# Depthwise convolution of a six-layer kernel: the taps as 128x32 column tiles over token-shifted copies

## The chip, the cores and the metric

The kernel runs on one core of a Trainium2 chip, as one program that computes six layers on 256 tokens. The metric is the time of one execution on the device, in microseconds (us): the median of the runs shown, less is better.

A core has five engines, each with its own queue of instructions that it works off in order: TensorE (PE, matrix products, with PEld for the loads of its stationary operand), VectorE (DVE), ScalarE (ACT), GpSimd (POOL) and SyncE (SP, here used to issue DMAs). They wait for one another by semaphores. Products land in PSUM, in one of eight banks of 128 partitions; everything else lies in SBUF, 128 partitions wide.

## The reference, cut to what matters

The first block has four layers: retention, convolution, dilated attention, retention, each followed by a SwiGLU of 2816 hidden features; a second block of two layers follows. The change touches the second layer alone, its mixer:

```python
def _conv_mixer(h, w_in, b_in, w_dw, b_dw, ln_g, ln_b, w_out, b_out):
    a = h @ w_in + b_in
    u = a[..., :D_MODEL] * jax.nn.sigmoid(a[..., D_MODEL:])
    u = lax.conv_general_dilated(
        u, w_dw[:, None, :].astype(u.dtype), window_strides=(1,), padding=[(CONV_PAD, CONV_PAD)],
        dimension_numbers=('NWC', 'WIO', 'NWC'), feature_group_count=D_MODEL) + b_dw
    u = jax.nn.silu(_layernorm(u, ln_g, ln_b))
    return u @ w_out + b_out
```

D_MODEL is 1024, there are 256 tokens, and the convolution is depthwise with 31 taps: for each channel c and token t the output is the sum over k of w_dw[k, c] * u[t + k - 15, c]. All of it is in 32 bit floating point.

## The kernel before

**Layout.** Activations lie transposed: channels on partitions, in eight chunks of 128, tokens along the free dimension. A weight matrix comes as a stream of 128x128 blocks in the order in which they are used; one DMA on SP's queue fetches 16 of them (`raw`, 1 MB, line 255, three buffers), and for each half tile ACT rounds to a high part (`hi`) and DVE subtracts to get a low part (`lo`). A product of a block is three matmuls (`mmB`, line 320): hi by the high part of x, hi by the low part, lo by the high part, each with 256 columns of fp32r. `_advance` (line 259) keeps the splits four half tiles and the loads five ahead of the half tile that is being used.

**Order.** Nothing is scheduled by a compiler. The program writes each engine's queue itself: a main line of products, and generators beside it (`spawn`, `pump`, `need`) that are resumed after each `mmB` once a planner's estimate of time has passed what they wait for. The planner has a cost for each operation (`Engine.cost`, `Kern.mm`). Where its estimate is wrong the order in the queues stays and the engine waits.

**The convolution layer** (`conv`, line 1056). `kouter` forms the products of w_in for chunks 0 to 2 over all of x; then the main line goes through chunks 3 to 7, 2 x 8 blocks each, that is 48 matmuls of one chunk. Each finished chunk has an `evac` (line 1071): GpSimd clears the padding of a tile `U`, DVE multiplies the products by the norm's factor R (`t`), ACT takes the sigmoid (`sg`), and DVE forms u in `U`, with 15 columns of padding on both sides, eight buffers.

The taps follow. For each chunk, 13 to 16 of the 31 go to TensorE (`TAPS`, line 1053): ACT builds a diagonal 128x128 matrix of the tap's weights for each (`cdg`, line 1098), and a matmul in fp32 of this matrix with `U` shifted by k columns is accumulated in a bank (`taps_pe`, line 1121). An fp32 matmul stands in the trace as two instructions. The other taps go to DVE, each one multiplying and adding along 256 tokens, into two accumulators `cv` and `cacc` in turn (`taps_dve`, line 1128); DVE then adds the two, and `combine` (line 1151) adds the bank.

`stats` (line 1160) subtracts a shift common to all channels, sums the channels and their squares (POOL adds chunk after chunk), and after the last chunk forms the layer norm's factors with PE, DVE and POOL in turn. `act` gives each chunk's silu as a high and a low part (`hh`, `hl`), and the main line goes on with w_out. Between the last tap and w_out, `warm` products, whose result nobody reads, keep PE occupied.

The constants of the channels, the 248 columns of tap weights among them, lie in the tile `V`, loaded at the start in two DMAs on ACT's queue (lines 423 and 438).

Of the kernel before, what the change touches and what calls it, by code (L numbers as in the profile page):

```python
# [19 lines left out]
D = 1024  # L20
# [11 lines left out]
# columns of the per-feature vectors, eight to a vector of 1024  # L32
# [3 lines left out]
def _vec_layout():  # L36
    n = 0
    for i in range(4):
        for j in range(4):
            VEC[f"n{i}{j}"] = n  # L40
            n += 8
    for name, w in (
        ("mix0", 8), ("mix1", 8), ("mlp0", 8), ("mlp1", 8), ("fin", 8),
        ("cb_in", 16), ("cb_dw", 8), ("cln_g", 8), ("cln_b", 8), ("cb_out", 8),
        ("lconv_w", 32), ("lconv_b", 8), ("lb_r", 8), ("lb_i", 8), ("lam", 8),
        ("mnorm", 8), ("subln", 1), ("cw_dw", 248),
    ):
        VEC[name] = n
        n += w
    return n  # L50
# [4 lines left out]
# columns of the scalars that every partition holds  # L55
# [8 lines left out]
def shape_consts():  # L64
# [23 lines left out]
    c["amask"] = mk  # L88
    c["cmask"] = np.where(s[None, :] <= s[:, None], 0.0, BIG).astype(f)
# [23 lines left out]

class Bank:
    """One bank of PSUM while it is held"""
# [8 lines left out]
class Times:  # L124
    """When the parts of the tensors will have been written, by an estimate of what every operation takes"""
# [24 lines left out]
class Engine:  # L150
    """An engine's operations, with the time it will have worked them off"""
# [51 lines left out]
class Kern:  # L203
    def __init__(self, nc, tc, ctx, ap, stop_after=None):
# [11 lines left out]
        # weight stream  # L216
# [6 lines left out]
        # chains beside the main line: [generator, time from which on it may go on]  # L223
# [12 lines left out]
        # whether an operation's start is held to be after the products that were given before it  # L236
# [10 lines left out]
    # ---------------------------------------------------------------- stream  # L247
    PD, PS = 5, 4

    def _load(self, n):  # L250
        """the next tile of the stream, in n pieces"""
# [25 lines left out]
    def blk(self, name, layer, r0, c0, n=1):  # L277
        """The next n 128x128 blocks (side by side along columns) of the stream, high and low part."""
# [13 lines left out]
    # -------------------------------------------------------------- products  # L292
# [6 lines left out]
    def mm(self, out, lhsT, rhs, start, stop):  # L299
# [3 lines left out]
        if rhs.dtype == F32:  # L303
            cost = 4 * max(n, 64) / 2400 if n > 8 else 0.2
        elif rhs.dtype == F32R:
            cost = max(n, 256) / 2400
        else:
            cost = max(n, 64) / 2400
# [7 lines left out]
    def w(self, *aps):  # L316
        """how long it will be until these have been written"""
        return max([self.times.read(x.t if isinstance(x, Bank) else x) for x in aps]) + 0.05 - self.now

    def mmB(self, out, w, xk, start, stop):  # L320
        """out[128 features, T] += block^T x; xk: (high, low) parts of x^T."""
# [7 lines left out]
    def mmA(self, out, w, xk, start, stop):  # L329
        """out[128 tokens, 512] += x block."""  # L330
# [7 lines left out]
    def warm(self, n):  # L338
        """Products that nobody reads, in a pause too short to let the array's clock drop."""
# [6 lines left out]
    # ------------------------------------------------- banks and side chains  # L346
# [61 lines left out]
    # ----------------------------------------------------------------- setup  # L408
# [46 lines left out]
    def log1p_series(self, s, shape, name, terms):  # L455
        """2 atanh(s), s an AP with |s| <= 1/3."""
# [11 lines left out]
    def softplus_tail(self, x, shape, name):  # L468
        """log1p(exp(-|x|))"""
# [11 lines left out]
    def decays(self):  # L481
        """log(1 - exp(l)) of every head, direction and layer"""
# [25 lines left out]
    def decay_tables(self, j, dp):  # L508
        """per head the blocks [later from earlier positions and the reverse; the two blocks on the diagonal]"""
# [16 lines left out]
    # ----------------------------------------------------------------- norms  # L526
# [6 lines left out]
    def sums(self, b, srcs, first, last):  # L533
        """columns 2 i and 2 i + 1 of b: what a sum over the channels of source i adds"""
# [6 lines left out]
    def rms_root(self, tiles, eps, ps):  # L541
        """(mean + eps)^-1/2 per token, tokens on partitions"""
# [13 lines left out]
    def bcast(self, rs, tiles, ps, o=0):  # L556
        """ps[p, t] = rs[t] on every partition"""
# [4 lines left out]
    def prenorm_chunk(self, c, src, gain, T, perm, have=False):  # L562
        """operand parts of src*gain (the high one may be there), and the sum of squares"""
# [21 lines left out]
    def prenorm_finish(self, T, tiles):  # L585
        """sets self.rs (tokens on partitions) and self.R (on every partition)"""
# [34 lines left out]
    def kouter(self, T, outs, key, cut=lambda n: 0):  # L621
        """Products of the first outputs of a projection, one chunk of x after the other.
        outs: (bank, column, first of its bank); key(k, n): block key; cut(n): tokens left out."""
# [17 lines left out]
    def splitp(self, src, T=T2):  # L641
        """high and low part of src (SBUF or PSUM) as tiles"""
# [6 lines left out]
    # ------------------------------------------ post norm of the first block  # L649
    OUT_TILES = ((0, 2), (2, 2), (4, 2), (6, 1), (7, 1))  # L650

    def out_alloc(self):
        """accumulators of the eight output chunks"""
# [17 lines left out]
    def post_begin(self, gain, nk, bias=None):  # L671
        """nk: products that are still to come for each chunk"""
# [6 lines left out]
    def post_chunk(self, c):  # L679
        """after the last product of chunk c"""  # L680
# [37 lines left out]
    def post_copy(self, c0, n, m, on_vector):  # L718
        """m * gain; the last on_vector of them on the vector engine"""
# [15 lines left out]
    def boundary(self, perm, gain2, perm2=False, full=False):  # L735
        """x += m * rstd * gain, then the operand of the next projection: its first chunk here, the others on
        the way (feed)"""
# [52 lines left out]
    def feed(self, n=1):  # L790
        """the next n chunks of the operand"""
# [4 lines left out]
    # ------------------------------------------------------------ first block  # L796
# [14 lines left out]
    def retention(self, i, j):  # L811
# [13 lines left out]
        # heads 0 and 1: queries and keys, one x chunk after the other  # L825
# [226 lines left out]
    # taps of each chunk of channels on the tensor engine  # L1052
    TAPS = (16, 13, 14, 16, 16, 16, 16, 14)
    CD = 1.0

    def conv(self, i, j):
# [8 lines left out]
        ln, U, sums = {}, {}, {}  # L1065
# [5 lines left out]
        def evac(c, b):  # L1071
# [3 lines left out]
            u = self.wk.tile([128, S + 30], F32, name="U", tag="U", bufs=8)  # L1075
# [13 lines left out]
            U[c] = u  # L1089

        def claim():
            """taps for the tensor engine, channel after channel, each with its diagonal matrix"""
            for c in range(KD):
                while c not in U:
                    yield None
                for k in range(self.TAPS[c]):
                    d = self.wk.tile([128, 128], F32, name="cdg", tag="cdg", bufs=8)
                    self.sc.activation(d, self.ident, AF.Copy, scale=self.vec("cw_dw", 8 * k + c))
                    yield c, k, d

        def taps_pe():
            src, ahead, b = claim(), deque(), None
            more = True
            while more or ahead:
                while more and len(ahead) < 4:
                    x = next(src, 0)
                    if x is None:
                        break
                    if x == 0:
                        more = False  # L1110
                    else:
                        ahead.append(x)
                if not ahead:
                    yield 0.3
                    continue
                c, k, d = ahead.popleft()
                last = k == self.TAPS[c] - 1
                if k == 0:
                    b, = yield from self.need(1)
                yield self.w(d, U[c])  # L1120
                self.mm(b[:, :S], d, U[c][:, k:k + S], k == 0, last)
                if last:
                    sums[c] = b
                    self.spawn(combine(c))
                if k % 2:
                    yield 0.0

        def taps_dve():
            for c in range(KD):
                while c not in U:  # L1130
                    yield 0.3
                shifted = "shift" in done
                if shifted:
                    done.add(("shifted", c))
                acc = [cv[:, c], self.wk.tile([128, S], F32, name="cacc", tag="cacc")]
                for n, k in enumerate(range(self.TAPS[c], 31)):
                    w = self.vec("cw_dw", 8 * k + c)
                    x, a = U[c][:, k:k + S], acc[n % 2]
                    if n == 0 and shifted:
                        self.ve.scalar_tensor_tensor(out=a, in0=x, scalar=w, in1=K, op0=ALU.mult, op1=ALU.subtract)  # L1140
                    elif n == 1 and not shifted:
                        self.ve.tensor_scalar(a, x, w, None, ALU.mult)
                    elif n < 2:
                        self.ve.tensor_scalar(a, x, w, self.vec("cb_dw", c), ALU.mult, ALU.add)
                    else:
                        self.ve.scalar_tensor_tensor(out=a, in0=x, scalar=w, in1=a, op0=ALU.mult, op1=ALU.add)
                    yield self.ve.clock - self.now - 0.5
                self.ve.tensor_tensor(acc[0], acc[0], acc[1], ALU.add)
                done.add(c)

        def combine(c):
            while c not in done:
                yield 0.1
            b = sums[c]
            yield self.w(b, cv[:, c]) + (0.0 if c == KD - 1 else self.CD)
            self.ve.tensor_tensor(cv[:, c], cv[:, c], b[:, :S], ALU.add)
# [3 lines left out]
        def stats():  # L1160
            """sums over channels, shifted by the mean of the first two chunks"""
# [89 lines left out]
        self.spawn(taps_pe())  # L1251
# [907 lines left out]
```

## Time and profile before

| | |
|---|---|
| Median of 3 runs | 2451.79 us (2450.5 to 2452.13) |
| Span of the profiled execution, first to last instruction | 2449.6 us |
| PE busy | 2398.2 us, 98 % of the span |
| DVE, ACT, POOL busy | 67 %, 47 %, 9 % |
| Mean granted TensorE clock | 0.998 |
| DMA | 384 MB read from HBM, 157 GB/s over the span |

The profiled execution's own span is 2.2 us under the median. The span runs from the first to the last instruction; what lies around it is in the run's time and not in the span. A matmul's end is modelled and lies after the start of the next one, so the pitch, from one start to the next, is what a stream of matmuls takes, and PE's busy share is not a measure of how well PE is used.

### The profile page before, as it was taken

The page shows a single profiled execution, that of the slowest core. Times are in us where ns is not written, and L with a number is a line of the kernel's source. Part 1 is how long each engine was busy: PE and PEld are TensorE (multiplying, and loading weights), DVE is VectorE, ACT ScalarE, POOL GpSimd, SP SyncE. Part 2 cuts the span into 40 slices and gives each one's busy share as a digit, 9 for nine tenths or more (in the row PEclk, how much of TensorE's full clock was granted, in tenths as well). Part 3 has the DMA queues.
Part 4 walks back from the last instruction along what each step waited for, and adds up shares of the span by engine and source line. Part 5 has one row for each costly group of instructions (what it writes and reads, how often), then busy time and mean ns, then how long its engine had stood idle before and what let it go on. Part 6 is the DMA issues. An engine that isn't in the chain of part 4 may idle for free.

```text
span 2449.6 us, 43712 instructions
## 1 busy us (share of the span) xinstructions
PE 2398.2 (98%) x18193; PEld 2284.9 (93%) x18193; DVE 1653.0 (67%) x2826; ACT 1162.2 (47%) x1879; POOL 224.1 (9%) x284
## 2 busy tenths in 40 slices
PE   7999999999999999999999999999999999999998
PEld 7889999989998989989998899999999999989998
DVE  7556756898567758777567557566776756586764
ACT  5544543665434444444445444344765444356443
POOL 1002001112002000020011002002000100131000
PEclk9999999999999999999999999999999999999999
DMA  6443553304554433325544453544343445433552
GB/s 240 161 172 125 214 184 138 146 34 161 190 184 156 152 141 136 116 108 211 186 149 176 155 186 144 205 173 161 135 154 138 157 170 182 168 112 113 206 190 104
DMA packets 56935, 387.89 MB, mean 158 GB/s; under 512 B 7360, under 2 KB 8128, under 8 KB 10656
## 3 DMA queue, kind: packets, MB, share of 16 engines
q1 hardware_dynamic: 53280, 381.18, 43.0%
q10 hardware_dynamic: 3200, 2.99, 0.4%
q8 instruction: 143, 2.34, 0.4%
q0 software_dynamic: 256, 0.92, 0.1%
q14 instruction: 56, 0.46, 0.1%
HBM read 384.02 MB, written 1.05 MB: 157 GB/s over the span
## 4 chain that ended last, share of the span: by engine, by line
PE 87%; DVE 6%; POOL 3%; issue 2%; ACT 2%; DMA 0%; ACTq 0%; SPq 0%; DVEq 0%; POOLq 0%
PE b L310 84%; DVE lo L198 2%; PE b L314 2%; POOL X L198 1%; ACT hi L198 1%; DVE cv L198 1%; POOL acc L198 1%; DVE xl L198 1%; DVE cacc L198 1%; POOL rs L198 1%; DVE xh L198 0%; PE b L343 0%; DVE ptmp L198 0%; DMA raw<-in_w 0%; DVE X L198 0%
## 5 line engine op out<-in xcount | busy, mean ns | idle before, releaser
L198 DVE TENSOR_TENSOR lo<-raw,hi 128x1024 fp32r<-128x1024 f32 (+1 forms) x723 | 876.6, 1235 | 278.7 <-ACT hi L198 278.6
L310 PE MATMUL b<-xh,hi 128*128 128x256 f32 (+1 forms) x3272 | 937.6, 290 | 14.3 <-ACT hi L198 9.3
L310 PE MATMUL b<-xl,hi 128*128 128x256 f32 (+1 forms) x3272 | 916.7, 284 | 4.3 <-DVE xl L198 4.1
L310 PE MATMUL b<-xh,lo 128*128 128x256 f32 (+1 forms) x3272 | 913.4, 283 | 0.9 <-DVE lo L198 0.9
L198 ACT CAST hi<-raw 128x1024 fp32r<-128x1024 f32 (+1 forms) x723 | 738.8, 1044 | 281.3 <-PE b L310 241.9
L310 PEld LDWEIGHTS b<-xh,hi 128*128 128x128 f32 x3272 | 611.2, 188 | 25.2 <-ACT hi L198 9.5
L310 PEld LDWEIGHTS b<-xl,hi 128*128 128x128 f32 x3272 | 611.0, 188 | 8.9 <-DVE xl L198 6.7
L310 PEld LDWEIGHTS b<-xh,lo 128*128 128x128 f32 x3272 | 613.4, 189 | 1.1 <-DVE lo L198 1.1
L310 PE MATMUL b<-hh,hi 128*128 128x256 f32 (+1 forms) x1792 | 511.1, 285 | 0.6 <-ACT hh L198 0.6
L310 PE MATMUL b<-hl,hi 128*128 128x256 f32 (+1 forms) x1792 | 507.4, 283 | 0.5 <-DVE hl L198 0.2
L310 PE MATMUL b<-hh,lo 128*128 128x256 f32 (+1 forms) x1792 | 507.1, 283 | 0.0
L310 PEld LDWEIGHTS b<-hh,hi 128*128 128x128 f32 x1792 | 337.5, 188 | 2.5 <-issue 0.9
L310 PEld LDWEIGHTS b<-hl,hi 128*128 128x128 f32 x1792 | 337.2, 188 | 1.7 <-DVE hl L198 1.3
L310 PEld LDWEIGHTS b<-hh,lo 128*128 128x128 f32 x1792 | 337.4, 188 | 0.0
L198 DVE TENSOR_TENSOR t<-b,R 128x512 f32<-128x512 f32 x96 | 65.4, 689 | 208.2 <-PE b L310 206.5
L310 PE MATMUL b<-hi,xh 128*128 128x512 f32 x352 | 142.2, 404 | 0.5 <-DVE xh L198 0.5
L310 PE MATMUL b<-lo,xh 128*128 128x512 f32 x352 | 140.0, 398 | 0.3 <-DVE lo L198 0.3
L310 PE MATMUL b<-hi,xl 128*128 128x512 f32 x352 | 139.6, 396 | 0.0
L198 ACT ACTIVATE sg<-t 128x256 f32<-128x256 f32 x88 | 36.5, 418 | 193.4 <-DVE t L198 193.2
L198 POOL TENSOR_TENSOR acc<-acc,sq 128x256 f32<-128x256 f32 (+1 forms) x90 | 83.0, 923 | 390.0 <-ACT sq L198 233.7
L198 POOL TENSOR_TENSOR psq<-psq 128x512 f32<-128x512 f32 x8 | 11.6, 1449 | 1014.3 <-ACT psq L198 1014.3
L198 ACT ACTIVATE sq<-X 128x256 f32<-128x256 f32 (+1 forms) x91 | 39.8, 439 | 117.6 <-POOL X L198 73.3
(313 smaller groups left out, 2179.3 us busy)
## 6 DMA issues: line engine op xcount, KB each, us to landing
raw<-in_w SPq DMA_DIRECT2D x359, 1024.0 KB, 4.8
raw<-in_w SPq DMA_DIRECT2D x4, 256.0 KB, 6.1
raw<-in_w SPq DMA_DIRECT2D x2, 512.0 KB, 9.9
dp<-in_c_dp SPq DMA_DIRECT2D x2, 512.0 KB, 4.6
wr<-in_lru_w SPq DMA_DIRECT2D x1, 1024.0 KB, 6.9
X<-in_x POOLq DMA_DIRECT2D x1, 640.0 KB, 9.6
c_rcs<-in_c_rcs ACTq DMA_DIRECT2D x2, 256.0 KB, 4.9
c_amask<-in_c_amask ACTq DMA_DIRECT2D x1, 512.0 KB, 3.6
```

Source lines behind the costliest of these rows:

```text
L198: return f(*args, **kw)
L310: self.nc.tensor.matmul(out, lhsT, rhs, start=start, stop=stop, skip_group_check=True)
L314: self.nc.tensor.transpose(out, in_, ident)
```

## The change

It does these things, all inside the convolution layer:

- DVE's taps, the two accumulators, the diagonal matrices on ACT and the division of the taps (`TAPS`) go. All 31 taps, filled up with a zero tap to 32, are done on TensorE.
- After `evac` has formed `U`, 16 DMAs on SP's queue copy it to a tile `cr` [128, 4, 284]. Each takes 32 channels (group g) and a shift a of 0 to 3 tokens: partitions 32a to 32a+31 of `cr[:, g]` hold the channels of group g, shifted by a.
- GpSimd builds for each chunk a tile `ctw` [128, 32, 32]: for each of 8 tap quartets q and 4 groups g a 128x32 matrix with the weights of four taps of one group, from a mask `m32` and a table `cwt`. These two are new constants, loaded on ACT's queue at the layer's start.
- A matmul of such a matrix contracts 128 rows (four taps by 32 channels) into 32 columns, the output partitions 32g to 32g+31 of the bank. 8 x 4 = 32 matmuls in fp32 with 256 columns make up a chunk; the four groups stand side by side in the array's columns. The planner is told 4.0 us for the 32 (`TAP`) and 7.5 us for the copies (`COPY`).
- `combine` adds the bias and subtracts the shift as it empties the bank, in one instruction (DVE where the shift is known, else ACT).
- `U` has three buffers in place of eight; `cr` and `ctw` have three each. `V` loses the 248 columns of taps.

```diff
+UW, RW = S + 31, S + 28
...
-    TAPS = (16, 13, 14, 16, 16, 16, 16, 14)
-    CD = 1.0
+    COPY, TAP = 7.5, 4.0
...
+        m32 = self.const("m32")
+        cwt = self.w1.tile([128, 256], F32, name="cwt")
+        nc.scalar.dma_start(out=cwt, in_=self.ap["cwt"])
...
-            u = self.wk.tile([128, S + 30], F32, name="U", tag="U", bufs=8)
+            u = self.wk.tile([128, UW], F32, name="U", tag="U", bufs=3)
...
             self.unlock("evac")
-            U[c] = u
+            r = self.wk.tile([128, 4, RW], F32, name="cr", tag="cr", bufs=3)
+            yield self.w(u) - 0.3
+            for g in range(4):
+                for a in range(4):
+                    nc.sync.dma_start(out=r[32 * a:32 * a + 32, g], in_=u[32 * g:32 * g + 32, a:a + RW])
+            self.times.write(r, max(self.now, self.times.read(u)) + self.COPY)
+            U[c] = r
...
-                    d = self.wk.tile([128, 128], F32, name="cdg", tag="cdg", bufs=8)
-                    self.sc.activation(d, self.ident, AF.Copy, scale=self.vec("cw_dw", 8 * k + c))
...
-                self.mm(b[:, :S], d, U[c][:, k:k + S], k == 0, last)
...
-                    else:
-                        self.ve.scalar_tensor_tensor(out=a, in0=x, scalar=w, in1=a, op0=ALU.mult, op1=ALU.add)
-                    yield self.ve.clock - self.now - 0.5
-                self.ve.tensor_tensor(acc[0], acc[0], acc[1], ALU.add)
...
+            w = self.wk.tile([128, 32, 32], F32, name="ctw", tag="ctw", bufs=3)
+            self.gp.tensor_tensor(w, m32[:, None, :].to_broadcast([128, 32, 32]),
+                                  cwt[:, 32 * c:32 * c + 32].unsqueeze(2).to_broadcast([128, 32, 32]), ALU.mult)
...
+            ws = {c: tapw(c) for c in range(2)}
             for c in range(KD):
                 while c not in U:
                     yield 0.3
+                yield self.w(U[c], ws[c])
+                b, = yield from self.need(1)
+                w = ws.pop(c)
+                for q in range(8):
+                    for g in range(4):
+                        self.mm(b[32 * g:32 * g + 32, :S], w[:, 4 * q + g], U[c][:, g, 4 * q:4 * q + S], q == 0, q == 7,
+                                TAP / 32)
+                if c + 2 < KD:
+                    ws[c + 2] = tapw(c + 2)
+                self.spawn(combine(c, b))
+                yield 0.0
...
+            if "shift" in done:
+                done.add(("shifted", c))
+                self.ve.scalar_tensor_tensor(out=cv[:, c], in0=b[:, :S], scalar=self.vec("cb_dw", c), in1=K,
+                                             op0=ALU.add, op1=ALU.subtract)
+            else:
+                self.sc.activation(cv[:, c], b[:, :S], AF.Identity, bias=self.vec("cb_dw", c))
```

## Rows read from the trace of the kernel before

**Rows 1.** Page, part 4: the chain that ended last, by engine.
```profile
PE 87%; DVE 6%; POOL 3%; issue 2%; ACT 2%; DMA 0%; ACTq 0%; SPq 0%; DVEq 0%; POOLq 0%
```
**Rows 2.** Windows: stretch, length, busy us (count) of PE PEld DVE ACT POOL, clock, DMA.
```profile
448.70:489.70 41.00, 41.00 (x282) 38.79 (x281) 36.58 (x76) 25.36 (x61) 2.28 (x4) 1.00 0.32 119
489.70:530.40 40.70, 36.70 (x170) 30.64 (x168) 40.42 (x92) 23.92 (x79) 8.53 (x10) 1.00 0.02 9
530.40:536.20 5.80, 5.71 (x46) 5.56 (x46) 2.27 (x9) 2.93 (x6) 0.71 (x1) 1.00 0.00 0
```
**Rows 3.** Instructions on tiles cdg and cv: count, ns min/median/max, first and last start.
```profile
L310 PE MATMUL b<-U,cdg x242: 377/378/483, 448.7 to 528.6; 128*128 128x256 f32 x121
L198 ACT ACTIVATE cdg<-c_ident,V x121: 384/386/405, 447.7 to 526.4; 128x128 f32<-128x128 f32 x121
L198 DVE SCALAR_TENSOR_TENSOR cv<-U,V,cv x59: 470/475/957, 452.7 to 529.0; 128x256 f32<-128x256 f32 x59
```
**Rows 4.** Timeline of PE, products and taps: start, us, instruction, idle time before, releaser.
```profile
450.01 0.28 PE L310 MATMUL b<-xl,hi 128*128 128x256 f32 x1
450.13 0.28 PE L310 MATMUL b<-xh,lo 128*128 128x256 f32 x1
...
489.72 11.82 PE L310 MATMUL b<-U,cdg 128*128 128x256 f32 x54
...
530.49 0.61 PE L310 MATMUL b<-onesD,cv 128*128 128x1 f32 x4 [1.50 <-DVE cv L198]
```
**Rows 5.** Timeline of DVE: two chunks' way to U, and the last sum.
```profile
447.43 0.49 DVE L198 SCALAR_TENSOR_TENSOR U<-t,V,sg 128x256 f32<-128x256 f32 x1 [0.35 <-ACT sg L198]
...
468.26 0.68 DVE L198 TENSOR_TENSOR t<-b,R 128x512 f32<-128x512 f32 x1
...
470.05 0.47 DVE L198 SCALAR_TENSOR_TENSOR U<-t,V,sg 128x256 f32<-128x256 f32 x1
...
530.01 0.42 DVE L198 TENSOR_TENSOR cv<-cv,b 128x256 f32<-128x256 f32 x1
```
**Rows 6.** Timeline, PE: products on 64 rows of the array, two narrow windows.
```profile
849.85 0.49 PE L310 MATMUL b<-aqk 64*128 64x128 f32 x4
...
849.86 0.49 PE L310 MATMUL b<-aqk 64*128 64x256 f32 x3
```
**Rows 7.** Timeline, PE: products into 64 columns of the array, and their neighbours.
```profile
842.51 0.28 PE L310 MATMUL b<-xh,lo 128*128 128x256 f32 x1
842.73 1.09 PE L310 MATMUL b<-pt,av 128*64 128x128 f32 x8
843.75 0.39 PE L310 MATMUL b<-xh,hi 128*128 128x256 f32 x1
```
**Rows 8.** Timeline of SP's queue, narrow windows: start and us of the DMA issues.
```profile
1262.26 0.33 SPq L819 DMA_DIRECT2D dp<-in_c_dp  x1
1262.64 0.42 SPq L255 DMA_DIRECT2D raw<-in_w  x1
...
0.75 0.39 SPq L255 DMA_DIRECT2D raw<-in_w  x1
1.19 0.90 SPq L255 DMA_DIRECT2D raw<-in_w  x2
```
**Rows 9.** DMA issues: KB each, median us from issue to landing.
```profile
raw<-in_w SPq DMA_DIRECT2D x359, 1024.0 KB, 4.8
...
c_tri<-in_c_tri ACTq DMA_DIRECT2D x1, 64.0 KB, 1.7
```
**Rows 10.** POOL's widest product, by tile: count, ns min/median/max, first and last start.
```profile
L198 POOL TENSOR_TENSOR psq<-psq x8: 1287/1488/1574, 213.6 to 1676.0; 128x512 f32<-128x512 f32 x8
```
**Rows 11.** Timeline of PE at its longest pause.
```profile
784.73 0.61 PE L310 MATMUL b<-onesD,acc 128*128 128x1 f32 x4 [2.16 <-POOL acc L198]
```
**Rows 12.** Window right behind it: length, PE busy (count), clock, DMA.
```profile
784.73:790.00 5.27, 4.99 (x16) 0.68 0.58 197
```
**Rows 13.** Timeline of ACT's queue at the attention layer's start: two constants' loads.
```profile
762.09 0.33 ACTq L411 DMA_DIRECT2D c_acs<-in_c_acs  x1
762.45 0.45 ACTq L411 DMA_DIRECT2D c_amask<-in_c_amask  x1
```

More of the change, by code (lines that the diff above doesn't have):

```diff
@@ L45, in _vec_layout @@
         ("lconv_w", 32), ("lconv_b", 8), ("lb_r", 8), ("lb_i", 8), ("lam", 8),
-        ("mnorm", 8), ("subln", 1), ("cw_dw", 248),
+        ("mnorm", 8), ("subln", 1),
     ):
@@ L88, in shape_consts @@
     c["amask"] = mk
+    c["m32"] = (s[:, None] % 32 == np.arange(32)[None, :]).astype(f)
     c["cmask"] = np.where(s[None, :] <= s[:, None], 0.0, BIG).astype(f)
@@ L297, in pe, with mm @@
         self.times.write(out, self.now + 0.06)
-    def mm(self, out, lhsT, rhs, start, stop):
+    def mm(self, out, lhsT, rhs, start, stop, cost=None):
         if isinstance(out, Bank):
@@ L302, in mm @@
         n = rhs.shape[-1]
-        if rhs.dtype == F32:
+        if cost is not None:
+            pass
+        elif rhs.dtype == F32:
             cost = 4 * max(n, 64) / 2400 if n > 8 else 0.2
@@ L1064, in conv @@
         self.ve.memset(self.ones256, 1.0 / 256)
-        ln, U, sums = {}, {}, {}
+        m32 = self.const("m32")
+        cwt = self.w1.tile([128, 256], F32, name="cwt")
+        nc.scalar.dma_start(out=cwt, in_=self.ap["cwt"])
+        ln, U = {}, {}
         done = set()
@@ L1088, in evac, with tapw, taps @@
             self.unlock("evac")
-            U[c] = u
[L1091 to L1096, printed above, removed]
-                    d = self.wk.tile([128, 128], F32, name="cdg", tag="cdg", bufs=8)
-                    self.sc.activation(d, self.ident, AF.Copy, scale=self.vec("cw_dw", 8 * k + c))
[L1099 to L1110, printed above, removed]
-                    else:
[L1112 to L1120, printed above, removed]
-                self.mm(b[:, :S], d, U[c][:, k:k + S], k == 0, last)
[L1122 to L1128, printed above, removed]
+            r = self.wk.tile([128, 4, RW], F32, name="cr", tag="cr", bufs=3)
[5 more added lines that the diff above has]
+            U[c] = r
+        COPY, TAP = self.COPY, self.TAP
+        def tapw(c):
+            w = self.wk.tile([128, 32, 32], F32, name="ctw", tag="ctw", bufs=3)
+            self.gp.tensor_tensor(w, m32[:, None, :].to_broadcast([128, 32, 32]),
+                                  cwt[:, 32 * c:32 * c + 32].unsqueeze(2).to_broadcast([128, 32, 32]), ALU.mult)
+            return w
+        def taps():
+            ws = {c: tapw(c) for c in range(2)}
             for c in range(KD):
@@ L1131, in taps_dve, with combine @@
                     yield 0.3
[L1132 to L1145, printed above, removed]
-                        self.ve.scalar_tensor_tensor(out=a, in0=x, scalar=w, in1=a, op0=ALU.mult, op1=ALU.add)
-                    yield self.ve.clock - self.now - 0.5
-                self.ve.tensor_tensor(acc[0], acc[0], acc[1], ALU.add)
[L1149 to L1156, printed above, removed]
+                yield self.w(U[c], ws[c])
[9 more added lines that the diff above has]
+                yield 0.0
+        def combine(c, b):
+            yield self.w(b)
+            if "shift" in done:
[4 more added lines that the diff above has]
+                self.sc.activation(cv[:, c], b[:, :S], AF.Identity, bias=self.vec("cb_dw", c))
             self.rel(b)
@@ L1250, in conv @@
             self.spawn(evac(c, B[c]))
-        self.spawn(taps_pe())
-        self.spawn(taps_dve())
+        self.spawn(taps())
         self.spawn(stats())
@@ L2109, in pack @@
     for a, b in (("cb_in", "conv_b_in"), ("cb_dw", "conv_b_dw"), ("cln_g", "conv_ln_g"), ("cln_b", "conv_ln_b"),
[L2110 removed]
+                 ("cb_out", "conv_b_out"), ("lconv_w", "lru_conv_w_2"),
                  ("lconv_b", "lru_conv_b_2"), ("lb_r", "lru_b_r_2"), ("lb_i", "lru_b_i_2"), ("lam", "lru_lambda_2"),
@@ L2114, in pack @@
     c["vec"] = v
+    w = np.zeros((32, D), np.float32)
+    w[:31] = f["conv_w_dw"][0]
+    c["cwt"] = np.ascontiguousarray(w.reshape(8, 4, 8, 4, 32).transpose(1, 4, 2, 0, 3).reshape(128, 256))
     row = np.concatenate([f["ret_log1m_decay"].reshape(-1), f["ab_if_bias_2"][0], f["c_lambda_2"][0].reshape(-1)])
```

1 line of the change is left out of this document (removed).

## The prediction

> **What bounds the kernel now.** I read the chain that ended last first: PE has 87 % of it, DVE 6 % [rows 1], so a change off PE pays only where PE stands still or does work that could go. Then I cut the convolution layer into windows. From 448.7 to 489.7 us PE is busy throughout and weights still stream in (DMA share 0.32): products of w_in and taps share the array. From 489.7 to 530.4 DMA falls to 0.02: 40.7 us in which no weight is used and nothing but taps is done, DVE at 40.42 of 40.70 us [rows 2]. So the layer waits there for taps, and DVE is the bound: at its end PE stood for 1.50 us until DVE had finished cv [rows 4], and DVE's last sum starts at 530.01 and takes 0.42 us [rows 5]. From then a chain of small steps to the first product of w_out takes 5.8 us [rows 2]; the change leaves it as it is. So the question is when the last chunk of cv is whole: at 530.4 before.
>
> PE is close behind DVE: 160 tap instructions lie in that stretch, of the 242 in all [rows 2, 3] (170 PE instructions in it, 10 of them sums). 54 in a row take 11.82 us [rows 4], 0.219 us each, so 160 take 35.0 of 40.7 us. Taking DVE's taps away alone would only hand the bound to PE.
>
> **What the taps cost on PE after.** A chunk has 32 matmuls, each two fp32 instructions of 256 columns as before: 64 passes. One after the other that is 64 x 0.219 = 14.0 us; with the four column groups side by side, 16 x 0.219 = 3.5 us. The trace has no four tiles side by side, so these are the ends. The nearest row is two tiles of 64 rows: the last products of one head start at 849.85 and the first of the next, in the other half of the array, at 849.86 [rows 6], 0.01 us apart where one tile's follow each other at 0.11 or more. So tiles do run side by side, though those share the rows and these the columns. I take four at a time. Going into and out of 64-column products costs: 842.51 to 842.73 is 0.22 where 0.12 is the pitch [rows 4, 7], and eight passes of half of 0.219 are 0.88 of the 1.02 us to 843.75 [rows 7]; together 0.24 us. T = 3.5 + 0.24 = 3.75 us a chunk, 30 us for eight, against 242 x 0.219 = 53 us before, and with all of DVE's taps in it.
>
> The Trainium skill ("TensorE: Matmul & The Clock Gate", section "Measured speedup vs the span model") has three column tiles at 2.38 times one, not 3. At that share four tiles would make 3.17, and T 4.66 us as an estimate from that page; about 3 us later at the end. No row here has column tiles together.
>
> **What the copies cost on SP.** 16 issues a chunk. Issues follow each other at 0.38 us (1262.26 to 1262.64) or 0.44 us (0.75 to 1.19), and the shortest takes 0.33 us [rows 8]; I take 0.38, the later one with the queue running. That is 6.1 us a chunk, 6.46 with the one weight load in it. Landing: 1.7 us for 64 KB, 4.8 us for 1 MB [rows 9]; a copy has 36 KB (32 x 284 x 4), I take 2.0 us. So a chunk's copies are there 8.1 us after its u, and SP can do no more than one chunk in 6.46 us, while PE needs only 3.75.
>
> **The walk.** A product's pitch is 0.118 us (450.01 to 450.13) [rows 4], a chunk's 48 take 5.66 us. In 448.7 to 489.7 the 82 taps (242 - 160) took 18.0 of 41.0 us, so 23.0 us of products remain at 448.7 [rows 2, 3]: chunk 3 has 0.4 left, chunks 4 to 7 5.66 each. From a chunk's last product to its u are 2.2 us (468.26 to 470.52 with DVE crowded) [rows 5].
> - u of chunk 0 is there at 447.9 [rows 5]; its copies land at 456.0, those of chunks 1 to 4 each 6.46 later: 462.5, 468.9, 475.4, 481.9. Each tap block starts then; that of chunk 4 ends at 485.6.
> - Products in the meantime: 7.3 us before 456.0, then little. The planner holds the copies to take 7.5 us each and doesn't know that they queue on SP, so it puts the tap blocks close together, with three or four products (1.1 to 1.4 us) between, and PE waits some 1.5 us at each. 7.3 + 4 x 1.2 = 12.1 of 23.0 us are done at 485.6.
> - Chunk 5's products are done by 485, its u at 487.3, its copies at 495.4. Chunk 6: 490.8, u at 493.0, behind chunk 5's copies, landed at 501.8. Chunk 7: 496.5, or 3.75 later if chunk 5's taps come first; u at 498.7 to 502.4, landed at 508.3 to 510.9.
> - Chunk 6's taps end at 505.6, so PE stands 2.7 to 5.3 us before chunk 7's. A pause of 2.16 us stood before 5.27 us at a mean granted clock of 0.68 [rows 11, 12]; that is 0.32 x 5.27 = 1.7 us lost to the lower of the two levels, 1.2 GHz. The last block ends at 513.8 to 516.4; 0.16 us until its last pass is out (377 ns against 219) and 0.48 us for DVE's one instruction [rows 3]: cv whole at 514.4 to 517.0, against 530.4. I take 515.5, 15 us earlier.
>
> **The rest of the edits.** ACT loses 121 x 0.386 = 47 us of diagonals [rows 3]; it wasn't the bound, so nothing. POOL gains eight products of 1024 columns: 512 take 1.49 us [rows 10], so 3.0 each, up to 6 if slowed; the first two are given before the first u, and the copies' landing hides them (else 3 us once). `U` with three buffers: DVE's u of chunk 3 (4) waits until the copies of chunk 0 (1) have landed, some 5 us; behind it on DVE stand the next `t` and the weights' low parts, for which PE's products would wait. Four half tiles of 24 products, 11 us, are split ahead: hidden, and PE waits for SP there anyway. The clearing of U's padding on POOL waits for the same. Weight loads on SP stand behind 16 copies, 6.1 us; five half tiles ahead are 14 us. SP's own wait for a `cr` buffer, chunk 3 for chunk 0's taps (459.8), is over when SP comes to it (467). Two loads of constants on ACT's queue at the layer's start: 0.33 + 0.45 us as in attention [rows 13], 0 to 0.8 in all, I take 0, as ACT is half idle. A shorter `V`: between 0 and half a microsecond gained, taken as 0.
>
> **Sum.** 15 us off the profiled 2449.6 us span; the median is 2.2 us above that span, and I hold that to stay: 2451.8 - 15 = 2437. Ends: if issues go at 0.33 and the planner's order fills PE without a pause, PE is the bound: 448.7 + 23.0 + 30 + 0.6 = 502.3, 28 us off, 2424. If issues take 0.45 and landing 4.8, the blocks of chunks 0 to 4 end at about 494, chunk 7's products at 505 and its copies at 519.5, cv at 525.6: 5 us off, 2447.
>
> **Rivals.**
> - *Column tiles don't run four at a time (slower or the same).* For it: they share each row's moving data, and the one overlap in the trace is of rows. Against: the array does take work for another tile while one is busy [rows 6]. With two at a time T = 7.25, and PE has 23.0 + 58 us without a pause: 530.3 at the least, 1 to 3 us later than before, 2453 to 2455. One at a time: 14.3, 448.7 + 23.0 + 114.4 + 0.6 = 586.7, 56 us later, 2508. It decides from T = 7.2 on.
> - *SP's issues are the bound (slower).* SP never rests: 447.9 + 136 issues + 2.0 + 3.75 + 1.7 + 0.6 passes 530.4 from 0.547 us an issue on; at twice 0.38 it is 559, 29 us later, 2481. Against: no issue in rows 8 comes 0.55 us behind the one before. The Trainium skill ("DMA: Bandwidth & Descriptors", section "Rules for kernel authors") says that under 64 KB one pays mostly overhead and should coalesce, which speaks against 128 copies. Were a landing of 1.7 us paid for each in turn, 128 would take 218 us; but 0.44 from issue to issue beside 4.8 to landing [rows 8, 9] shows them overlapped.
> - *The gain is eaten by the chain of the last chunk.* The copies' 8 us lie on the path where DVE took chunks at once; if PE pauses cost the lower clock at each of five blocks (1.7 each) and landing is slow, 2447 to 2451: no change.
>
> **Chances.** The forecast's own range, 2424 to 2447, has 0.72; another 0.05 lies below. The same within 0.2 % (about 5 us, what a measurement of this kernel can tell from no change): 0.11, two at a time or a gain that is eaten. Slower by more: 0.12, one tile at a time 0.07, SP 0.05. The range 2424 to 2456 holds the first and the third: 0.83. Faster 0.77, same 0.11, slower 0.12.
>
> **What would show it.** Right: the 64 passes of a chunk start within about 3.7 us, four at a time; `cacc` and `cdg` are gone; SP issues 16 copies in 6 us, back to back from 448 to 480; PE waits there for DMA, and once for 2 to 5 us before the last block, with a lower clock behind it; the stretch without weights shrinks from 40.7 to below 25 us. Wrong: passes at 0.2 us each in a single line; copies more than 0.5 us apart; low parts of weights late on DVE, with PE waiting for `lo`; or a pause in the 5.8 us behind the last cv that wasn't there.

## The result: 23 us slower, and the profile after

| | before | after |
|---|---|---|
| Median in the runs taken side by side | 2451.14 us | 2474.08 us (2473.51 to 2476.78, 4 runs) |
| Ratio to before | | 1.0096, 95 % interval 1.0082 to 1.011 |
| Span of the profiled execution | 2449.6 us | 2471.7 us |
| Mean granted TensorE clock | 0.998 | 0.990 |

The forecast was 15 us faster. Its own landmarks say where it went wrong: cv was to be whole at 515.5 us; before it was at 530.4 [rows 5], now it is at 553.05 (the end of DVE's last instruction on it, begun at 552.56). The layer is the only place: from the norm's factor just ahead of it (`rs`, at 416.52 before and 415.82 after) to the first sum for silu (`hf`) it takes 117.7 us before and 141.2 after, 23.5 us more, and that is the whole difference.

Windows of the kernel after, core 0, the stretches that answer to [rows 2]: length, busy us (count) of PE, PEld, DVE, ACT, POOL, granted clock, DMA share, GB/s.

```profile
447.99:490.00 42.01, 31.78 (x300) 21.61 (x298) 8.47 (x12) 4.87 (x8) 7.98 (x10) 0.88 0.29 78
490.00:530.00 40.00, 26.51 (x286) 19.81 (x286) 11.20 (x17) 9.36 (x17) 11.09 (x16) 0.83 0.31 94
530.00:553.04 23.04, 15.27 (x132) 7.31 (x132) 0.96 (x2) 0.42 (x1) 1.41 (x2) 0.70 0.54 175
553.04:559.03 5.99, 5.99 (x51) 5.80 (x50) 2.26 (x10) 2.96 (x6) 0.71 (x1) 1.00 0.01 3
```

Now no computing engine is busy throughout: DVE, at 40.42 of 40.70 us before, has 11.20 of 40; PE 26.51 of 40. So the bound is to be looked for in a queue that the busy columns don't count. The last row, from the whole cv to the first product of w_out, is nearly as it was (5.99 against 5.80). SP's timeline is the one that is nearly full: start, us, DMA issues.

```profile
448.08 21.70 SPq L1101 DMA_DIRECT2D cr<-U  x32
469.88 0.53 SPq L259 DMA_DIRECT2D raw<-in_w  x1
470.51 21.82 SPq L1101 DMA_DIRECT2D cr<-U  x32
492.44 0.52 SPq L259 DMA_DIRECT2D raw<-in_w  x1
493.13 21.24 SPq L1101 DMA_DIRECT2D cr<-U  x32
514.47 0.52 SPq L259 DMA_DIRECT2D raw<-in_w  x1
524.21 10.01 SPq L1101 DMA_DIRECT2D cr<-U  x16
534.33 0.52 SPq L259 DMA_DIRECT2D raw<-in_w  x1
535.02 10.71 SPq L1101 DMA_DIRECT2D cr<-U  x16
```

32 copies take 21 to 22 us: 0.66 to 0.68 us each with the few that take over 1 us, where the forecast had 0.38. From 448.08 SP rests once, from 514.99 to 524.21. The tiles by themselves (count, ns min/median/max, first and last start, then issue to landing):

```profile
L316 PE MATMUL b<-cr,ctw x512: 376/379/637, 457.3 to 552.1; 128*32 128x256 f32 x171
L1101 SPq DMA_DIRECT2D cr<-U x128: 507/589/1532, 448.1 to 545.1; - x128
DMA to landing us min/median/max: 1.8/1.9/5.5
```

An issue itself takes 589 ns; the shortest, 507, is over the 0.33 to 0.45 of [rows 8]. From one copy's start to the next the median is 0.633 us (0.634 below, as in what was expected), the mean 0.67, since some issues take over 1 us. Who stood for it, from the waits of the kernel after (us in total, times, longest):

```profile
ACT hi L202 <- DMA raw<-in_w: 45.2, 3, 24.2
DVE lo L202 <- ACT hi L202: 41.0, 6, 17.3
POOL U L202 <- DMA cr<-U: 32.0, 3, 13.8
PE b L316 <- DMA cr<-U: 21.2, 12, 2.8
PE b L316 <- ACT cv L202: 10.2, 1, 10.2
DVE U L202 <- DMA cr<-U: 7.9, 1, 7.9
```

Two readings fit these lines: the copies are late because SP issues too slowly, or the weights are late because their loads (three between 448 and 524) stand behind 32 copies each. The runs tell them apart.

### The profile page after: what moved, and what is told of

Same layout as the page of the kernel before. It is cut to its first block, busy times and chain, and to the rows that moved or that the text cites. A ratio compares the mean times of both kernels' runs of the same rounds, so it can differ in the third digit from the quotient of the medians.

```text
span 2471.7 us, 44255 instructions
## 1 busy us (share of the span) xinstructions
PE 2397.4 (97%) x18463; PEld 2267.6 (92%) x18463; DVE 1597.6 (65%) x2688; ACT 1128.0 (46%) x1762; POOL 236.0 (10%) x292
## 4 chain that ended last, share of the span: by engine, by line
PE 70%; DVE 3%; POOL 2%; issue 2%; ACT 1%; SPq 1%; DMA 0%; ACTq 0%; DVEq 0%; POOLq 0%
PE b L316 68%; PE b L320 1%; POOL X L202 1%; DVE lo L202 1%; POOL acc L202 1%; ACT hi L202 1%; DVE xl L202 1%; SPq L1101 1%; POOL rs L202 0%; PE b L349 0%; DVE xh L202 0%; DVE ptmp L202 0%; DVE X L202 0%; DMA raw<-in_w 0%; ACT psq L202 0%
```

## The experiments

Times are medians; each batch was compared with runs of the kernel before on the same chip (2451.71, 2450.95 and 2454.43 us).

**1. The copies without DMAs (x1_engines).**

```diff
-                    nc.sync.dma_start(out=r[32 * a:32 * a + 32, g], in_=u[32 * g:32 * g + 32, a:a + RW])
-            self.times.write(r, max(self.now, self.times.read(u)) + self.COPY)
+                    d, s = r[32 * a:32 * a + 32, g], u[32 * g:32 * g + 32, a:a + RW]
+                    if a % 2:
+                        self.sc.copy(d, s)
+                    else:
+                        self.ve.tensor_copy(d, s)
```

The planner's 7.5 us for a chunk's copies goes with the DMAs; it now reckons with the copies on DVE and ACT.

> The 128 shifted copies are done by DVE (shifts 0 and 2) and ACT (shifts 1 and 3) instead of DMAs on SP; all else as after the change. Theory Q (the loss is SP's queue: copies issued 0.634 us apart, and weight loads behind them): both go, a copy of 32x284 on DVE or ACT costs 0.2 to 0.4 us, 8 on each engine 2 to 3 us a chunk, PE becomes the bound, weights arrive in time: 2423 to 2438 us. Theory T (128x32 tiles and their clock are what costs): no better than 2465.

Measured: 2435.23 us, ratio 0.9934 (0.9919 to 0.9948), 39 us under the changed kernel, cv whole at 515.63. The instructions on `cr` in this run:

```profile
L202 ACT COPY cr<-U x64: 423/426/432, 450.7 to 511.0; 32x284 f32<-32x284 f32 x64
L202 DVE COPY cr<-U x64: 289/300/1958, 452.9 to 510.1; 32x284 f32<-32x284 f32 x64
```

ACT makes such a copy in 426 ns and DVE in 300; SP takes 589 to ask for it. So the loss is in how the copies are made; the taps on TensorE are not at fault. The planner's other reckoning is in the 39 us too; run 5, which leaves it as it was, gets 32 of them.

**2. The weights off SP's queue (x2_weights_act), and the planner told the copies' real time (x5_weights_planner).** In the first the layer's weight loads go on ACT's queue and the copies have SP to themselves; the second adds a planner that knows that copies queue.

```diff
-            self.nc.sync.dma_start(out=t[:, c], in_=self.ap["w"][self.n_dma][:, c])
+            self.wq.dma_start(out=t[:, c], in_=self.ap["w"][self.n_dma][:, c])
...
+        self.wq = nc.scalar
```

> Weight loads of the convolution layer are issued on ACT's queue, the copies stay alone on SP. Theory Q1 (weights late behind 32 copies are the whole loss): ACT's waits for raw of 45 us go, PE is fed, 2437 us. Theory Q2 (the issue pitch of 0.634 us alone, 128 x 0.634 = 81 us of SP): last copies land at 448 + 81 + 2 = 531, cv whole at about 537 against 552.6 after and 530.4 before: 2457 to 2460. Theory T: unchanged, 2474.

```diff
-    COPY, TAP = 7.5, 4.0
+    COPY, TAP = 10.4, 4.0
...
-            self.times.write(r, max(self.now, self.times.read(u)) + self.COPY)
+            self.copied = max(self.copied, self.now, self.times.read(u)) + self.COPY
+            self.times.write(r, self.copied + 2.0)
```

> As x2, and the planner is told what the copies take: one chunk after the other, 10.4 us each, landing 2 us later, in place of 7.5 us each by itself. Theory P (a part of the loss is that PE's order puts taps in front of products that could run): 5 to 15 us under x2, PE's pauses before taps gone, its clock full. If SP's 81 us are the bound whatever the order: within 3 us of x2.

Measured: 2477.44 us (ratio 1.0105, 1.0089 to 1.012) and 2471.91 (1.0081, 1.0064 to 1.0098). ACT's wait for `raw` fell from 45.2 to 11.0 us in the first (445 to 556 us), and the time rose by 3.4. A part of that is a price of the edit itself: the first u comes 4.6 us later (452.63 against 447.99), as the loads now stand in ACT's queue. But from the first copy to the whole cv it is still 104.1 us against 105.0, so the reading that late weights are the loss falls. SP's timeline in the two, one line each, first of x2_weights_act, then of x5_weights_planner:

```profile
452.78 96.74 SPq L1103 DMA_DIRECT2D cr<-U  x128
```
```profile
452.17 91.95 SPq L1104 DMA_DIRECT2D cr<-U  x128
```

Both still need over 90 us for 128 copies. The first numbers expected for moving the weights (2457 to 2460, cv at 537) missed too: cv was whole at 556.84. They took 128 x 0.634 = 81 us with no rest; SP began 4.8 us later, issues that took longer than that made about 7 us more, and SP rested 8.5 us again before chunk 6 (519.8 to 528.3). In this run that rest doesn't come from late weights: on PE the last products of chunk 6 stand behind the tap blocks of chunks 4 and 5, which wait for copies. In the changed kernel weights had a hand in it, as its timelines of ACT and PE show:

```profile
497.87 1.04 ACT L202 CAST hi<-raw 128x1024 fp32r<-128x1024 f32 x1 [17.13 <-DMA raw<-in_w]
...
499.34 1.01 PE L316 MATMUL b<-ones,cv 128*128 128x1 f32 x4 [10.18 <-ACT cv L202]
```

PE's longest pause, 10.18 us, is for a step of cv that stands in ACT's queue behind this rounding. How SP's rest divides there between weights and order, no run separates. With the planner told, 5.5 us come back, the lower end of theory P: from the first copy to the whole cv it is 98.9 us, and SP's copies take 92 of them, a rest of 3.7 us included. The order matters, at second rank.

**3. Two queues (x3_two_queues).** Odd shifts on ACT's queue, even ones on SP's.

```diff
-                    nc.sync.dma_start(out=r[32 * a:32 * a + 32, g], in_=u[32 * g:32 * g + 32, a:a + RW])
+                    (nc.sync, nc.scalar)[a % 2].dma_start(out=r[32 * a:32 * a + 32, g], in_=u[32 * g:32 * g + 32, a:a + RW])
```

> Copies of odd shifts go on ACT's queue, those of even shifts stay on SP with the weights. If an issue costs its own queue alone 0.59 us, the copies of a chunk take 5.1 us and the weights wait half as long: 2440 to 2450, with ACT's roundings of the weights up to 5 us late. If the two queues share what takes the time, the pitch over both stays 0.634 and the time stays at 2470 to 2476.

Measured: 2454.03 us, ratio 1.001 (1.0001 to 1.002), 4 us over what was expected. The issues in this run:

```profile
L1101 SPq DMA_DIRECT2D cr<-U x64: 507/592/1817, 449.2 to 526.6; - x64
L1101 ACTq DMA_DIRECT2D cr<-U x64: 514/606/1569, 449.2 to 526.9; - x64
```

Both queues issue at the same time at the price that one has alone, so in this run it is a price of each issuing engine and not of something that the two share. But ACT pays it out of its own time: 64 x 0.606 = 39 us, and a copy that it would make in 0.426 us. `sg` and `hi` stood 14.6 and 11.2 us behind copies; u of chunk 6 came at 511.95. The Trainium skill ("DMA: Bandwidth & Descriptors", section "Issuing engines are not separate DMA queues") says that several issuing engines save only the time to initiate, usually small beside the transfer. That the time to initiate is what is saved, these lines bear out; it was not small: 20 us of 2474.

**4. What the price hangs on (x6_forms).** Chunk 1: each copy in two of half the columns; chunk 2: each in two of half the rows; chunk 5: twelve more DMAs.

```diff
+                    if c == 1:
+                        for h in range(2):
+                            nc.sync.dma_start(out=d[:, 142 * h:142 * h + 142], in_=s[:, 142 * h:142 * h + 142])
...
+                for n in range(4):
+                    nc.sync.dma_start(out=f[:, n], in_=u[:, 0:128])
+                for n in range(4, 8):
+                    nc.sync.dma_start(out=f[0:32, n], in_=self.ap["w"][0][0:32, 0:128])
+                for n in range(8, 12):
+                    nc.sync.dma_start(out=f[:, n], in_=self.ap["w"][0][:, 0:128])
```

> The changed kernel, with copies of other forms in three chunks and twelve further DMAs that nobody reads (their targets aren't used; the result is the same). It asks what the cost of an issue on SP's queue hangs on, so only durations of issues are read, not the time. Chunks 0, 3, 4, 6, 7: the 16 copies as they are, 32 partitions x 284 columns from SBUF to SBUF, 0.59 us each as in the changed kernel. Chunk 1: each copy cut into two of 32 partitions x 142 columns. Chunk 2: each copy cut into two of 16 partitions x 284 columns. Chunk 5: beside its 16 copies four DMAs SBUF to SBUF of 128 partitions x 128 columns, four from HBM to SBUF of 32 partitions x 128, four from HBM to SBUF of 128 partitions x 128. Theory P (an issue costs by the number of its rows, one for each partition): 0.59 in chunk 1, about 0.4 to 0.5 in chunk 2, well over 1 us for the forms of 128 partitions. Theory B (by bytes): 0.3 to 0.5 in chunks 1 and 2 alike, over 0.8 for 128 x 128 columns (64 KB against 36). Theory S (by where the source lies, SBUF or HBM): 0.55 to 0.63 in chunks 1 and 2 and for 128 partitions from SBUF, 0.33 to 0.45 for all eight from HBM. Theory R (the queue is full, and an issue waits until an earlier one has been worked off): the first few after a pause take 0.33 to 0.4, those behind them 0.59, whatever their form.

Measured, by line: half the columns; half the rows; the copies as they are; 128 x 128 from SBUF; 32 x 128 from HBM; 128 x 128 from HBM.

```profile
L1104 SPq DMA_DIRECT2D cr<-U x32: 523/588/595, 459.0 to 478.6; - x32
L1107 SPq DMA_DIRECT2D cr<-U x32: 507/587/1267, 479.9 to 500.3; - x32
L1110 SPq DMA_DIRECT2D cr<-U x96: 507/588/1210, 448.2 to 571.7; - x96
L1114 SPq DMA_DIRECT2D f<-U x4: 592/599/601, 533.5 to 535.5; - x4
L1116 SPq DMA_DIRECT2D f<-in_w x4: 419/506/1012, 536.1 to 538.3; - x4
L1118 SPq DMA_DIRECT2D f<-in_w x4: 422/430/432, 538.7 to 540.2; - x4
```

18 KB cost what 64 KB cost, 16 rows what 128 do: the theories of rows and of bytes fall. From HBM it is 0.42 to 0.43 us once the copies are past (the first two behind them took 0.59 and 1.01), from SBUF 0.59. A full queue isn't it either: the first copy of chunk 6, after 9.2 us of rest, took 0.562. So among these forms theory S holds. But the source alone isn't it. All kernels end with stores from SBUF to HBM; in the kernel before:

```profile
2444.03 0.35 SPq L2056 DMA_DIRECT2D out<-fo  x1
...
2445.21 0.34 SPq L2056 DMA_DIRECT2D out<-fo  x1
```

Their source is in SBUF, and they take little more than a lone load from HBM (0.33), while a copy behind a rest takes 0.507 to 0.596. So what costs more is a DMA with both ends in SBUF; whether it is that or something else that goes with such a DMA, no run shows. With the issues of two chunks doubled (32 more) and the twelve others, this one execution took 2499.78 us.

**5. The forecast's own price, restored (x7_ten).** Ten of the 16 copies on SP, three on DVE, three on ACT.

```diff
-                    nc.sync.dma_start(out=r[32 * a:32 * a + 32, g], in_=u[32 * g:32 * g + 32, a:a + RW])
+                    d, s = r[32 * a:32 * a + 32, g], u[32 * g:32 * g + 32, a:a + RW]
+                    n = 4 * g + a
+                    if n < 10:
+                        nc.sync.dma_start(out=d, in_=s)
+                    elif n % 2:
+                        self.sc.copy(d, s)
+                    else:
+                        self.ve.tensor_copy(d, s)
```

> The changed kernel with 10 of each chunk's 16 copies as DMAs on SP's queue and the other six as instructions, three on DVE and three on ACT. The planner is told the same as in the changed kernel. Ten issues at the measured 0.634 us take 6.3 us a chunk, which is what the prediction assumed for all sixteen (6.1), while the rest of its walk stays as it is: if only the issue's cost was mis-sized, the forecast's own number should come back, 2437 us +- 6, with cv whole at 513 to 519 us, SP resting between chunks from chunk 4 on, and tap blocks that wait little. If the time stays at 2450 or more, something else in the walk was wrong too (the planner's order, weights behind the copies, POOL's products), and the windows of PE's waits tell which. If the three copies each on DVE and ACT cost by themselves, the run with all copies on DVE and ACT (2435) bounds that: no worse than 2440 by them alone.

Measured: 2441.82 us (2440.95 to 2443.1), ratio 0.9964 (0.995 to 0.9978), cv whole at 519.43. SP's timeline, its first chunks and the last:

```profile
448.05 13.32 SPq L1104 DMA_DIRECT2D cr<-U  x20
461.47 0.53 SPq L259 DMA_DIRECT2D raw<-in_w  x1
462.10 7.18 SPq L1104 DMA_DIRECT2D cr<-U  x10
469.38 0.53 SPq L259 DMA_DIRECT2D raw<-in_w  x1
470.22 20.32 SPq L1104 DMA_DIRECT2D cr<-U  x30
...
507.50 6.27 SPq L1104 DMA_DIRECT2D cr<-U  x10
```

The first four chunks begin 448.05, 455.13, 462.10, 470.22 and the fifth 477.31: 7.3 us a chunk, not quite the 6.46 wanted, which makes 3.4 us at chunk 4. Its tap block ends at 489.45 where the walk has 485.6 (3.9 later), cv is whole 3.9 after the forecast's 515.5, and the time is 4.8 above 2437. So with SP's time for a chunk nearly what was assumed, the walk ends where it said, late by what the copies still cost too much and by about 1 us more.

**6. Ten copies, and the weights on ACT's queue (x9_ten_wact).** The edit of 2 on top of that of 5.

```diff
+        self.wq = nc.scalar
```

> The run with ten of a chunk's 16 copies on SP (2441.8 us, 4.8 above the forecast), and beside that the layer's weight loads issued on ACT's queue in place of SP's. In the run with ten copies the weight load at 490.59 us stood behind 30 copies that SP issued from 470.22 on; ACT's rounding to hi waited for raw for 15.3 us in two places, and u of chunk 6 came at 500.35, where the forecast's walk has it at 493.0. Theory H (the step that held the weight loads to be hidden behind the copies is what is left of the miss): ACT's wait for raw falls below 4 us, u of chunk 6 comes before 496, cv is whole by 516, and the time is 2434 to 2438. Theory O (the rest is the order that the planner wrote, or the copies still late): within 2 us of 2441.8, with ACT's wait gone and PE waiting for copies as before. Theory A (ACT is hurt by issuing, its roundings and sigmoids come behind loads that wait for a buffer): 2443 to 2450, with ACT standing at its queue's loads.

Measured: 2449.48 us, ratio 0.9974 (0.9964 to 0.9983), 0.001 above run 5's, some 2.5 us, though the two intervals overlap. The first u came 5.7 us later (453.71 against 447.97), as the layer's first loads now stand in ACT's queue; from there to the whole cv it is 72.9 us against 71.5. ACT's waits from the first copy on, first of run 5, then of this one (us in total, times, longest):

```profile
ACT hi L202 <- DMA raw<-in_w: 15.3, 2, 12.5
```
```profile
ACT hi L202 <- DMA raw<-in_w: 2.0, 2, 1.5
```

Behind the copies the wait for `raw` did go, from 15.3 to 2.0 us (another 10.5 us of it arose ahead of the first copy), and nothing was gained by it: from the first u to that of chunk 6 it is 52.5 us against 52.4. So theory H falls: as far as this run tells, what the weights waited behind run 5's copies (10 to 30 of them) was hidden. From the first u on it is theory O; ahead of it loads on ACT's queue make the layer begin later, as in run 2, which is nearer to theory A. The 1.4 us that the 3.4 of run 5 leave of its 4.8 stay unexplained.

**7. POOL's matrices from HBM (x8_host_taps).** The run of 1, with `ctw` loaded ready made in place of POOL's eight products.

```diff
-            self.gp.tensor_tensor(w, m32[:, None, :].to_broadcast([128, 32, 32]),
-                                  cwt[:, 32 * c:32 * c + 32].unsqueeze(2).to_broadcast([128, 32, 32]), ALU.mult)
+            nc.sync.dma_start(out=w, in_=self.ap["ctw"][c])
+            self.times.write(w, self.now + 5.0)
```

> The run with all copies on DVE and ACT, and beside that the matrices of taps (ctw) loaded from HBM ready made, 512 KB a chunk in one DMA on SP's queue, in place of POOL's product of mask and table: 8 POOL instructions of 1.92 us and the two constants' loads are gone, eight DMA issues are added. In the run with all copies on DVE and ACT eight DVE copies took 2.5 us, but 5.6 to 6.9 where POOL worked on ctw or on the sums at the same time. Theory C (POOL's products slow DVE's copies, and that lies on the path): 2428 to 2433, with DVE's copies at 0.30 us each beside where ctw stood. Theory N (what DVE loses there is hidden, since PE has other work): 2434 to 2437, the same as with POOL's products. If the loads of 512 KB come late or push the weights back, slower: 2438 to 2442, with PE waiting for ctw or DVE for hi.

Measured: 2426.97 us (2425.65 to 2427.37), ratio 0.9901 (0.9886 to 0.9916), cv whole at 506.79: 24 us faster than before and 47 faster than the changed kernel, the best of all. The timelines of DVE and of POOL in the run of 1 show the place:

```profile
452.87 2.53 DVE L202 COPY cr<-U 32x284 f32<-32x284 f32 x8
456.04 5.59 DVE L202 COPY cr<-U 32x284 f32<-32x284 f32 x8
...
455.66 1.92 POOL L202 TENSOR_TENSOR ctw<-c_m,cwt 128x1024 f32<-128x1024 f32 x1
459.24 1.91 POOL L202 TENSOR_TENSOR ctw<-c_m,cwt 128x1024 f32<-128x1024 f32 x1 [1.67 <-PE b L316]
```

and the same copies with the matrices from HBM:

```profile
447.55 2.54 DVE L201 COPY cr<-U 32x284 f32<-32x284 f32 x8
455.65 2.53 DVE L201 COPY cr<-U 32x284 f32<-32x284 f32 x8
...
484.95 3.53 DVE L201 COPY cr<-U 32x284 f32<-32x284 f32 x8
```

Eight copies take 2.53 us alone and 5.59 beside two of POOL's products; the slowest copy, 1958 ns, lasts as long as such a product (1.92 us). Without them only POOL's sums, from 484.52 on, still cost one group 1 us. The Trainium skill ("SBUF — State Buffer", section "Who interferes with whom") has DVE, in instructions of some kinds, and GpSimd share a pair of ports that one holds for a whole instruction while the other stands; these rows agree. The gain, 8.3 us by the medians, is a little over the 2 to 7 expected. In the profiled executions the layer, from the norm's factor ahead of it to the whole cv, takes 97.2 us in run 1 and 90.8 here, 6.4 less; run 1's execution came to the layer 2.4 us later. The planner's price for `ctw` and the order on PE moved with it, and how much is due to that wasn't separated.

## Why the prediction was wrong, step by step

- **The bound before** was read rightly: with DVE's taps gone and the copies made cheaply, cv is whole 15 to 24 us earlier (515.63 and 506.79 against 530.4).
- **T, a chunk's taps on PE: right.** Forecast 3.75 us. The timeline of PE after, a block that waits for nothing, and its beginning in a narrow window:

```profile
508.74 0.28 PE L316 MATMUL b<-xh,lo 128*128 128x256 f32 x1
508.95 3.66 PE L316 MATMUL b<-cr,ctw 128*32 128x256 f32 x64
512.54 0.39 PE L316 MATMUL b<-xh,hi 128*128 128x256 f32 x1
```
```profile
508.95 0.85 PE L316 MATMUL b<-cr,ctw 128*32 128x256 f32 x12
```

  From 508.74 to 512.54 are 3.80 us, less the one product's 0.12: 3.68. Four passes start 7 ns apart and the next four 0.22 us on. The rival of column tiles that don't run four at a time falls with its argument, that they "share each row's moving data": here each of the four has an operand of its own, and they overlap all the same. And the trace does not agree with the 4.66 us estimated from the Trainium skill ("TensorE: Matmul & The Clock Gate", section "Measured speedup vs the span model"): the 14.0 us estimated for a single line became 3.5 side by side, four tiles at four times.
- **SP's issue: the step that failed.** "I take 0.38, the later one with the queue running": measured 0.634, or 0.67 in the mean, for 128 issues 32 to 37 us more. Rows 8 hold loads from HBM alone; no DMA in the trace of before goes from SBUF to SBUF, and the text put a price of another kind of transfer on it without saying so, and gave it a narrow upper end (0.45). Size was not the trap, as run 4 shows, nor a source in SBUF alone, but a DMA from SBUF to SBUF. Run 1, without these DMAs, gives 39 us back, and run 5, with ten in place of sixteen, 32. The argument against the rival, "no issue in rows 8 comes 0.55 us behind the one before", had the same hole.
- **The rival that came true** was there, "SP's issues are the bound", with its threshold at 0.547 us, and a chance of 0.05. Its own formula at the measured 0.634 gives 447.9 + 136 x 0.634 + 8.05 = 542.2, 12 us late; SP's rest before chunk 6 adds 9.2, to 551.4, against 553.05 measured. That rest was missing in the rival too: when copies are late, the products of chunk 6, written behind the tap blocks, are late with them (and in this kernel late weights add to it, see 2).
- **Landing**, 2.0 forecast, 1.9 measured: right. The rule of the Trainium skill ("DMA: Bandwidth & Descriptors", section "Rules for kernel authors"), that small transfers should be coalesced, pointed the right way; what was paid for each was its issue, not its landing.
- **The walk** otherwise: right at its end, within 1.4 us of what the price left over explains (run 5), but not at every step, so this is in part luck. There u of chunk 6 came at 500.35 and not at 493.0, because its last products stood behind chunk 5's taps; chunk 7's copies began 5.1 us after the walk's latest (507.50 against 502.4), and their taps ended 11.4 us behind that beginning where the walk has 14.0.
- **Weight loads behind the copies: "hidden"** was wrong in the changed kernel (ACT stood 45.2 us for `raw`), since they stood behind 32 copies, 21 us, and not 16, 6.1. But it was not what bound it: taken away, it gave 1 us between the first copy and the whole cv (run 2). In run 5, where they stood behind 10 to 30 copies, the 15.3 us that ACT stood for them cost nothing that run 6 could get back.
- **`U`'s three buffers**: DVE's u stood 7.9 us for copies, once, against 5 forecast; a consequence of the same price.
- **POOL's product**, 3.0 forecast, was 1.91 us; that it slows DVE's work beside it was not in the text. What it costs the changed kernel, where DVE is nearly idle, no run tested; in the version that gives DVE the copies it is 6 to 8 us.
- **The clock**: 1.7 us were set aside for the last block, and that was right: from the last copy's landing (545.14 and 1.85 us, 547.0) to the whole cv are 6.0 us, against 3.75 + 1.7 + 0.6. After, PE's pauses are longer: in 530.00:553.04 the mean granted clock is 0.70, and the block begun at 501.13, behind the pause of 10.2 us, took 5.8 us against 3.28 from its first pass to its last. The pauses come from late copies and, that one, from weights late behind copies; the clock isn't a cause of its own.

## What to carry to other kernels

Price a DMA's issue from a row with the same source and target, and where there is none, give it an upper end wide enough that a rival with a known threshold (here 0.547) lies inside it. Count issues against the queue that makes them, since no busy column shows it: when no computing engine is busy throughout and one queue's timeline is nearly solid, look there first, and take its work off it to see. For small moves between partitions, compare the issue with doing the move: an instruction of 0.30 or 0.43 us beat an issue of 0.59.

## What was not expected of the hardware

- An issue of a DMA from SBUF to SBUF takes 0.59 us (0.634 from one to the next), whatever its size between 18 and 64 KB and its rows between 16 and 128; from HBM it is 0.42 to 0.43 in a row and 0.33 alone, from SBUF to HBM 0.34 to 0.35 alone. SP and ACT pay it each for itself, at the same time.
- Four column tiles of 32 in fp32 run wholly side by side: 64 passes of 256 columns in 3.28 us from the first start to the last.
- A DVE copy of 0.30 us stretched to 1.96 us beside a POOL product of 1.92 us.
